# An interleave kernel on one core: rows of 32 KiB in double buffers, loads issued from GpSimd with joined descriptors asked for

## The chip, the cores and the metric

The kernel runs on one core of a Trainium2 chip. The metric is device time in microseconds, the median of several executions. The profile's span is shorter than this time by 1.8 to 2.6 us. Ratios are the mean time of one kernel's fast runs over that of the other's fast runs of the same rounds, so they are not quite the ratios of the medians quoted.

## The reference

```python
batch, seq, dim = 32, 256, 1024
# x, y: float32 (batch, seq, dim)
result[..., 0::2] = x
result[..., 1::2] = y        # float32 (batch, seq, 2 * dim)
```

No arithmetic is done: 67.11 MB are read and 67.11 MB written, in another order.

## The kernel before

The flat arrays are cut into tiles of 128 rows. SyncE issues the loads of x and y, VectorE copies each into every second element of an output tile, ScalarE issues the store.

```python
WL = 4096                    # columns of a load tile: rows of 16 KiB
WS = 2048                    # columns of x per output tile: output rows of 16 KiB
xpool = ctx.enter_context(tc.tile_pool(name="xp", bufs=3))
ypool = ctx.enter_context(tc.tile_pool(name="yp", bufs=3))
opool = ctx.enter_context(tc.tile_pool(name="op", bufs=6))
lwidths = [WL] * (total // P // WL - 1) + [2048, 1024, 512, 256, 256]
for lw in lwidths:
    ...
    nc.sync.dma_start(out=xtile, in_=xs)
    nc.sync.dma_start(out=ytile, in_=ys)
    while soff < lw:
        ...
        nc.vector.tensor_copy(out=otile[:, 0::2], in_=xsub)
        nc.vector.tensor_copy(out=otile[:, 1::2], in_=ysub)
        nc.scalar.dma_start(out=os_, in_=otile)
```

The last widths shrink, so that little stands alone at the end: the last load, its copies, the last store.

Of the kernel before, what the change touches and what calls it, by code (L numbers as in the profile page):

```python
# [2 lines left out]

# [4 lines left out]


@with_exitstack
def kernel(
    ctx: ExitStack,
    tc: tile.TileContext,
    x: bass.AP,
    y: bass.AP,
    out: bass.AP,
):
    nc = tc.nc
    P = 128  # L20

    total = 1
    for s in x.shape:
        total *= s

    WL = 4096
    WS = 2048

    xf = x.rearrange("b s d -> (b s d)")
    yf = y.rearrange("b s d -> (b s d)")  # L30
    of = out.rearrange("b s d -> (b s d)")

    fp32 = mybir.dt.float32

    xpool = ctx.enter_context(tc.tile_pool(name="xp", bufs=3))
    ypool = ctx.enter_context(tc.tile_pool(name="yp", bufs=3))
    opool = ctx.enter_context(tc.tile_pool(name="op", bufs=6))

    lwidths = [WL] * (total // P // WL - 1) + [2048, 1024, 512, 256, 256]
    assert sum(lwidths) == total // P  # L40

    start = 0
    k = 0
    for lw in lwidths:
        xtile = xpool.tile([P, WL], fp32, name="xtile")[:, :lw]
        ytile = ypool.tile([P, WL], fp32, name="ytile")[:, :lw]

        xs = dataclasses.replace(xf, offset=start, ap=[[lw, P], [1, lw]])
        ys = dataclasses.replace(yf, offset=start, ap=[[lw, P], [1, lw]])
        nc.sync.dma_start(out=xtile, in_=xs)  # L50
        nc.sync.dma_start(out=ytile, in_=ys)  # L51

        soff = 0
        while soff < lw:
            width = min(WS, lw - soff)
            otile = opool.tile([P, 2 * WS], fp32, name="otile")[:, : 2 * width]
            os_ = dataclasses.replace(
                of,
                offset=2 * start + 2 * soff,
                ap=[[2 * lw, P], [1, 2 * width]],  # L60
            )
            xsub = xtile[:, soff : soff + width]
            ysub = ytile[:, soff : soff + width]
            if False:
                nc.gpsimd.tensor_copy(out=otile[:, 0::2], in_=xsub)
                nc.gpsimd.tensor_copy(out=otile[:, 1::2], in_=ysub)
            else:
                nc.vector.tensor_copy(out=otile[:, 0::2], in_=xsub)  # L68
                nc.vector.tensor_copy(out=otile[:, 1::2], in_=ysub)  # L69
            nc.scalar.dma_start(out=os_, in_=otile)  # L70
            k += 1
            soff += width

        start += P * lw
    assert start == total


# [1 line left out]
_INS = ['x', 'y']  # L79
_OUTS = [((32, 256, 2048), 'float32')]  # L80


# [23 lines left out]
```

## Time and profile before

| | before |
|---|---|
| time, median (four runs) | 319.75 us |
| span of the profiled run | 317.6 us |
| first data packet, last packet ends (us into the span) | 1.73, 315.96 |
| DMA bytes, mean rate | 134.24 MB, 423 GB/s |
| VectorE busy | 24% |

The rows of the page that carry the bound stand in the prediction below. Between the first and the last packet lie 314.2 us. So nearly all of the time is data moving, and 3.4 us of the span are start and end. The chances of a change lie in the cost per packet (8.4 ns by the prediction's fit), in these edges, and in not making holes.

### The profile page before, as it was taken

The numbers are of one execution on the slowest core, as the hardware profiler recorded it, in microseconds if no ns is written. First come the engines' busy times: TensorE is split into PE (matmuls) and PEld (weight loads), VectorE is DVE, ScalarE is ACT, GpSimd is POOL, SyncE is SP. The second block draws the span as 40 slices with busy tenths as digits, with TensorE's granted clock in tenths as the row PEclk, the third lists the DMA queues.
The fourth block names the chain that finished last, engine by engine and source line by source line (L and its number), as shares of the span: only waits on it lengthen the run. The fifth ranks groups of instructions, "written<-read, shape, count | busy, mean of one in ns | idle before, by whom it ended". The sixth has DMA issues, their size and how long they took to land.

```text
span 317.6 us, 285 instructions
## 1 busy us (share of the span) xinstructions
DVE 76.8 (24%) x70; POOL 0.2 (0%) x4
## 2 busy tenths in 40 slices
DVE  0522112222022221122220222202222202221130
POOL 0000000000000000000000000000000000000000
DMA  8999999999999999999999999999999999999997
GB/s 293 429 396 429 429 431 429 429 429 437 437 435 433 433 429 429 429 429 429 429 431 429 429 429 435 437 437 430 431 431 429 431 429 429 429 432 427 421 423 285
DMA packets 10802, 134.24 MB, mean 423 GB/s; under 512 B 1200, under 2 KB 1712, under 8 KB 2608
## 3 DMA queue, kind: packets, MB, share of 16 engines
q1 hardware_dynamic: 5760, 67.11, 50.0%
q10 hardware_dynamic: 5040, 67.11, 49.4%
q14 instruction: 2, 0.02, 0.0%
HBM read 67.11 MB, written 67.11 MB: 423 GB/s over the span
## 4 chain that ended last, share of the span: by engine, by line
DMA 94%; issue 3%; SPq 1%; DVE 1%
DMA xtile<-in_x_dram 82%; DMA ytile<-in_y_dram 12%; SPq L51 0%; DVE otile L69 0%; SPq L50 0%; DVE otile L68 0%
## 5 line engine op out<-in xcount | busy, mean ns | idle before, releaser
L68 DVE COPY otile<-xtile 128x2048 f32<-128x2048 f32 (+3 forms) x35 | 38.4, 1134 | 118.4 <-issue 94.4
L69 DVE COPY otile<-ytile 128x2048 f32<-128x2048 f32 (+3 forms) x35 | 38.4, 1134 | 117.9 <-DMA ytile<-in_y_dram 117.9
L90 POOL MEMSET const-bfloat16-1.0<- 128x1 bf16 x1 | 0.1, 102 | 0.0
L90 POOL MEMSET const-uint8-127<- 128x1 uint8 x1 | 0.1, 101 | 0.0
L90 POOL MEMSET const-float32-0.0<- 128x1 f32 x1 | 0.1, 99 | 0.2 <-issue 0.2
L90 POOL MEMSET const-float32-1.0<- 128x1 f32 x1 | 0.1, 98 | 0.0
## 6 DMA issues: line engine op xcount, KB each, us to landing
out_dram<-otile ACTq DMA_DIRECT2D x31, 2048.0 KB, 19.5
xtile<-in_x_dram SPq DMA_DIRECT2D x15, 2048.0 KB, 38.8
ytile<-in_y_dram SPq DMA_DIRECT2D x15, 2048.0 KB, 38.8
xtile<-in_x_dram SPq DMA_DIRECT2D x1, 1024.0 KB, 36.4
ytile<-in_y_dram SPq DMA_DIRECT2D x1, 1024.0 KB, 34.0
out_dram<-otile ACTq DMA_DIRECT2D x1, 1024.0 KB, 9.2
xtile<-in_x_dram SPq DMA_DIRECT2D x1, 512.0 KB, 29.0
ytile<-in_y_dram SPq DMA_DIRECT2D x1, 512.0 KB, 30.2
```

The source lines that it names most:

```text
L68: nc.vector.tensor_copy(out=otile[:, 0::2], in_=xsub)
L69: nc.vector.tensor_copy(out=otile[:, 1::2], in_=ysub)
L90: nc = _bacc.Bacc("TRN2", target_bir_lowering=False, num_devices=1)
```

## The change

The intent: longer rows mean fewer descriptors; the memory stays the same (192 KiB per partition) because triple and sixfold buffering become double; loads leave SyncE for GpSimd, where `single_packet=True` asks for descriptors to be joined.

```diff
-    WL = 4096
-    WS = 2048
+    WL = 8192
+    WS = 4096
...
-    xpool = ctx.enter_context(tc.tile_pool(name="xp", bufs=3))
-    ypool = ctx.enter_context(tc.tile_pool(name="yp", bufs=3))
-    opool = ctx.enter_context(tc.tile_pool(name="op", bufs=6))
+    xpool = ctx.enter_context(tc.tile_pool(name="xp", bufs=2))
+    ypool = ctx.enter_context(tc.tile_pool(name="yp", bufs=2))
+    opool = ctx.enter_context(tc.tile_pool(name="op", bufs=2))
...
-    lwidths = [WL] * (total // P // WL - 1) + [2048, 1024, 512, 256, 256]
+    lwidths = [WL] * (total // P // WL - 1) + [4096, 2048, 1024, 512, 512]
...
-        nc.sync.dma_start(out=xtile, in_=xs)
-        nc.sync.dma_start(out=ytile, in_=ys)
+        nc.gpsimd.dma_start(out=xtile, in_=xs, single_packet=True)
+        nc.gpsimd.dma_start(out=ytile, in_=ys, single_packet=True)
```

(A counter and a branch that was never taken are removed too; they leave no instruction.)

More of the change, by code (lines that the diff above doesn't have):

```diff
@@ L33 @@
     fp32 = mybir.dt.float32
-    xpool = ctx.enter_context(tc.tile_pool(name="xp", bufs=3))
-    ypool = ctx.enter_context(tc.tile_pool(name="yp", bufs=3))
-    opool = ctx.enter_context(tc.tile_pool(name="op", bufs=6))
-    lwidths = [WL] * (total // P // WL - 1) + [2048, 1024, 512, 256, 256]
+    xpool = ctx.enter_context(tc.tile_pool(name="xp", bufs=2))
+    ypool = ctx.enter_context(tc.tile_pool(name="yp", bufs=2))
+    opool = ctx.enter_context(tc.tile_pool(name="op", bufs=2))
+    lwidths = [WL] * (total // P // WL - 1) + [4096, 2048, 1024, 512, 512]
     assert sum(lwidths) == total // P
     start = 0
-    k = 0
     for lw in lwidths:
@@ L63 @@
             ysub = ytile[:, soff : soff + width]
-            if False:
-                nc.gpsimd.tensor_copy(out=otile[:, 0::2], in_=xsub)
-                nc.gpsimd.tensor_copy(out=otile[:, 1::2], in_=ysub)
-            else:
-                nc.vector.tensor_copy(out=otile[:, 0::2], in_=xsub)
-                nc.vector.tensor_copy(out=otile[:, 1::2], in_=ysub)
+            nc.vector.tensor_copy(out=otile[:, 0::2], in_=xsub)
+            nc.vector.tensor_copy(out=otile[:, 1::2], in_=ysub)
             nc.scalar.dma_start(out=os_, in_=otile)
-            k += 1
             soff += width
```

## The prediction

> **What bounds the kernel now.** I read the page's first three parts, then the stretches of the span (windows), the order of instructions in the middle (timeline), what DVE waits for, and last the single packet records of the DMA queues in the trace.
>
> ```profile
> DVE 76.8 (24%) x70; POOL 0.2 (0%) x4
> DMA  8999999999999999999999999999999999999997
> GB/s 293 429 396 429 429 431 429 429 429 437 437 435 433 433 429 429 429 429 429 429 431 429 429 429 435 437 437 430 431 431 429 431 429 429 429 432 427 421 423 285
> q1 hardware_dynamic: 5760, 67.11, 50.0%
> q10 hardware_dynamic: 5040, 67.11, 49.4%
> ```
>
> The row DMA is the busy share of the 16 DMA engines in tenths, 40 slices of the span. It is full in all slices but the first and the last, and the rate under it stays near 430 GB/s. Queue q1 holds the loads, q10 the stores: 50.0% and 49.4% add up to 99.4% of the engines' time. VectorE works 24% of the span. So the kernel is bound by DMA, without holes to fill.
>
> ```profile
> 100.00:200.00 100.00, 23.64 (x20) 0.00 (x0) 1.00 1.01 432
> 200.00:290.00 90.00, 22.51 (x19) 0.00 (x0) 1.00 1.00 430
> 310.00:318.00 8.00, 0.29 (x1) 0.00 (x0) 1.00 0.68 276
> ```
>
> The last two columns are DMA share and GB/s: 1.00 or 1.01 in the long middle. Only the last 8 us are partly empty (0.68).
>
> ```profile
> 57.75 0.33 SPq L50 DMA_DIRECT2D xtile<-in_x_dram  x1
> 57.77 2.36 DVE L68 COPY otile<-xtile 128x2048 f32<-128x2048 f32 x2 [7.42 <-issue]
> 67.44 2.37 DVE L69 COPY otile<-ytile 128x2048 f32<-128x2048 f32 x2 [7.31 <-DMA ytile<-in_y_dram]
> ```
>
> VectorE does two copies of x in 2.36 us, then is idle over 7 us until y is there. Its waits are the consequence of the DMA bound, not a cause.
>
> **The floor, from packet sizes.** In the trace a packet of 1 KiB took 46 ns, 2 KiB 84, 4 KiB 159, 8 KiB 309, 16 KiB 611 (medians, alike in both queues). The slope is (611-46)/(16384-1024) ns per byte, or 27.2 bytes per ns; the rest is 611-602.6 = 8.4 ns for each packet. A semaphore write is a packet of its own, 9 ns. One engine carries 8 of a tile's 128 rows. Before: 40 loads and 35 stores, 75 DMAs x 8 rows = 600 data packets per engine. Bytes: 134.22 MB/16/27.2 = 308.4 us; fixed: 600 x 8.4 ns = 5.0 us; semaphores: 75 x 9 ns = 0.7 us; together 314.1 us. In the trace the first data packet starts 1.7 us into the span and the last packet ends at 316.0: 314.2 us. The model fits and there is no idle in it. The remaining 1.7 us are the end of the program. The reported 319.8 us is 2.2 us above the span of 317.6.
>
> [...]16 x 27.2 bytes per ns is 435 GB/s, and 430 is reached with the packets' fixed cost in it.[...] q1 and q10 each get half.[...] Here the first SyncE load was issued at 0.73 us and moved at 1.73, so 1.0 us; nothing in this trace shows GpSimd.[...] The copies do run[...] (2048 elements in 1225 ns, 1024 in 697: 0.52 ns per element)[...].
>
> **The change, part by part.** The bytes are the same. *Rows of 32 KiB:* now 12 widths, so 24 loads, and 14+5 = 19 stores; 43 DMAs x 8 = 344 row descriptors per engine instead of 600. Fixed cost 344 x 8.4 ns = 2.9 us and semaphores 0.4 us: DMA work 308.4+2.9+0.4 = 311.7 us, a gain of **2.4 us**. If joined descriptors share one fixed cost, the loads' 192 x 8.4 ns = 1.6 us goes too, at most. *VectorE:* half the instructions of double size; about 1225 + 2048 x 0.52 = 2290 ns each, 4.6 us for an x and y pair. It stays at a quarter of the span.[...]
>
> *Double buffers:* the middle worked as a timetable. Loads have run ahead and wait; two output buffers are being stored, and store A ends at time 0. Store B then occupies the engines until 9.7. Meanwhile VectorE sees A's semaphore (0.4 us, as the first x load's last semaphore write to its copy, 8.09 to 8.48 us), refills A (4.6), and the new store's first packet starts about 1.4 us after (estimate, a bit above SyncE's 1.0 at the start): 6.4 us. So there is always a store to move, with 3.3 us to spare. When B is refilled too, x and y come free and two loads follow[...]. A period is 4 x 9.7 = 38.8 us for 16 MiB, without a hole. The engines' spread at the end of a load or store is up to 1.9 us in the trace (27.71 to 29.61 us for the semaphore writes of the first store), which leaves 1.4 us. **No idle in the middle, but thin.**
>
> *Tail:* the last stores of 4096, 2048, 1024, 512, 512 columns go through two buffers, no longer six. If the 4096 one ends at T, those of 2048 and 1024 end at T+4.9 and T+7.3. The next needs the buffer of the 2048 one: 4.9+0.4+0.9 (two short copies)+1.4 = T+7.6, so 0.3 us of idle; it ends at T+8.9. The last needs the buffer freed at T+7.3: +2.7 = T+10.0, 1.1 us more. With the spread between engines I take **+2.5 us**. The end of the program stays 1.7 us.
>
> Sum: 3.0 + 311.7 + 2.5 + 1.7 = 318.9 us of span, + 2.2 = **321.1 us**. I round up to 321.5 for small holes in the middle.
>
> **Rivals.** *A: no buffer stall at all, only the gain in descriptors.* The fit of 314.1 against 314.2 speaks for it; the later start and the two output buffers against. It makes 319.8-2.4 = 317.4 us, or 316 with the joined fixed cost. Even this is not 2% faster (313.4), as the bytes alone need 308.4 us. *B: the double buffer becomes the wait.* Slack is 3.3 us per period[...]. There are about 7 periods; 2 us lost in each makes 14 us, about 335 us. For it speaks the arithmetic of thin slack[...]; against it that stores are always queued at the boundaries in my timetable. *C: GpSimd's path is slower itself*[...]: 2% on the loads' half costs 3 us, about 325. [...]I hold it unlikely.
>
> **Range and chances.** A and the plain sum span 316 to 322, a mild B or C reaches 328. I give 318 to 328 for 8 in 10. Faster by 2% would need DMA above 435 GB/s or nearly so: 0.02. Slower by 2%, above 326.2 us, needs B or a strong C: 0.19. Else the same: 0.79.
>
> **What the changed profile would show.** Right: DMA at 9 in all middle slices, at most 2 or 3 us of holes, all near the end; 32 KiB packets of 1.21 us; loads and stores alternating in bursts rather than half and half; first packet near 3 us; VectorE still near 25%, now waiting for output buffers (stores) rather than for y. Wrong: slices of 7 or 8 in the middle once per 38.8 us (B), packets longer than 1.22 us or one DMA engine behind the others (C), or a start later than 4 us. What would overturn it most is loads crowding out stores so that the two output buffers stand waiting while the loads have nowhere to land.

The prediction's sum came to 3.0 + 311.7 + 2.5 + 1.7 = 318.9 us of span, 321.1 us of time, rounded up to 321.5. Its first term: a start at 3.0 us, 1.3 later than the 1.7 of before. An assumption changed no term of the sum, only the order: that loads from GpSimd take longer turns than stores and so run ahead. The timetable of the double buffers starts from it. Its 9.7 us for a load or a store are 8 rows of 1.213 us (32768 bytes at 27.2 per ns, and 8.4 ns).

## The result, and the profile after

The changed kernel takes **321.64 us** (321.47 to 321.81, four runs) against 319.75 us: ratio 1.0059, 95% interval 1.0045 to 1.0074. That is 1.9 us slower, and "the same" at 2%. The profiled run has a span of 319.1 us.

The page of the changed kernel: busy time of the compute engines, DMA share and rate in 40 slices, queues (q0 now holds the loads).

```profile
DVE 73.6 (23%) x38; POOL 22.6 (7%) x28
DMA  6999999999999999999999999999999999999996
GB/s 263 456 419 370 448 419 444 448 411 448 415 448 448 407 448 415 448 448 411 448 415 444 444 419 448 415 444 431 431 448 411 429 431 439 458 423 413 396 379 250
q0 software_dynamic: 3200, 67.11, 49.4%
q10 hardware_dynamic: 2736, 67.11, 49.1%
```

The DMA row is 9 everywhere but at the edges, as before; the first slice fell from 8 to 6, the last from 7 to 6. The last three rates (396, 379, 250) are lower than those of before (421, 423, 285). A single slice of the middle says little: a row of 1.2 us is booked where it starts.

What engines wait for, changed kernel:

```profile
POOL xtile L49 <- DVE otile L63: 258.7, 9, 44.6
DVE otile L63 <- DMA out_dram<-otile: 182.3, 15, 23.5
DVE otile L64 <- DMA ytile<-in_y_dram: 35.4, 10, 7.6
```

VectorE now waits mostly for output buffers, that is for stores to finish (182.3 us in 15 waits), no longer for y. With the DMA engines full (share 1.00 from 40 to 240 us, below) this waiting costs nothing by itself.

To see where time came from, take the same stretches of both kernels. Columns: stretch and length, busy time of VectorE and of GpSimd with instruction counts, clock, DMA share, GB/s. First the kernel before:

```profile
3.00:40.00 37.00, 11.18 (x10) 0.00 (x0) 1.00 1.00 421
40.00:240.00 200.00, 47.91 (x41) 0.00 (x0) 1.00 1.01 431
240.00:290.00 50.00, 13.05 (x11) 0.00 (x0) 1.00 1.00 428
290.00:300.00 10.00, 1.23 (x1) 0.00 (x0) 1.00 1.01 429
300.00:310.00 10.00, 3.08 (x7) 0.00 (x0) 1.00 1.02 415
310.00:315.00 5.00, 0.29 (x1) 0.00 (x0) 1.00 1.01 413
```

Then the changed kernel:

```profile
3.00:40.00 37.00, 8.99 (x4) 1.55 (x3) 1.00 0.99 414
40.00:240.00 200.00, 45.45 (x20) 12.78 (x10) 1.00 1.00 433
240.00:290.00 50.00, 13.68 (x6) 3.62 (x4) 1.00 1.01 433
290.00:300.00 10.00, 1.23 (x1) 0.54 (x1) 1.00 0.97 414
300.00:310.00 10.00, 2.62 (x3) 2.15 (x3) 1.00 0.99 376
310.00:315.00 5.00, 1.36 (x4) 0.00 (x0) 1.00 0.94 389
```

The rates show where to look: less at the start, a little more in the middle, less after 290 us, where the tiles shrink (the tail). For amounts they are too coarse, as the view books a row where it starts, and one row of 32 KiB on each of 16 engines is 0.5 MB, or 1.2 us. So the packet records of both traces were counted, each row by the part of it that had moved. Put into time at 431 GB/s, the changed kernel is 0.9 us behind at 40 us and 0.3 us ahead at 290 us. Its last packet ends 1.6 us later (317.57 against 315.96 us). So the start lost about 0.9 us, the middle won about 1.1, and **the tail lost about 1.9 us**. Counted from the end, the last 10 MB took 26.2 us, in the kernel before 24.3.

Two details of the changed kernel's trace. First, GpSimd's issues beside a copy, in the middle (start, length, engine; in brackets the idle time before it and what ended it):

```profile
73.32 2.29 DVE L64 COPY otile<-ytile 128x4096 f32<-128x4096 f32 x1
73.70 2.02 POOL L49 DMA_DIRECT2D xtile<-in_x_dram  x1 [44.64 <-DVE otile L63]
75.91 0.53 POOL L50 DMA_DIRECT2D ytile<-in_y_dram  x1 [0.18 <-issue]
```

GpSimd is free to issue x's load at 73.70, when the copy of x is done, but VectorE is copying y until 75.61; GpSimd's instruction ends 0.11 us after that and lasts 2.02 us, where the undisturbed one lasts 0.53. All six issues of the trace that met a copy of 4096 columns lasted 2.02 to 2.03 us. They cost nothing visible here: from 40 to 240 us the rate is 433 GB/s, as in the run with loads from SyncE.

Second, the tail:

```profile
301.09 1.23 DVE L64 COPY otile<-ytile 128x2048 f32<-128x2048 f32 x1 [7.64 <-DMA ytile<-in_y_dram]
302.39 0.69 DVE L63 COPY otile<-xtile 128x1024 f32<-128x1024 f32 x1
303.59 0.69 DVE L64 COPY otile<-ytile 128x1024 f32<-128x1024 f32 x1 [0.50 <-DMA ytile<-in_y_dram]
310.25 0.43 DVE L63 COPY otile<-xtile 128x512 f32<-128x512 f32 x1 [5.97 <-DMA out_dram<-otile]
310.69 0.43 DVE L64 COPY otile<-ytile 128x512 f32<-128x512 f32 x1
314.49 0.43 DVE L63 COPY otile<-xtile 128x512 f32<-128x512 f32 x1 [3.38 <-DMA out_dram<-otile]
314.84 0.42 DVE L64 COPY otile<-ytile 128x512 f32<-128x512 f32 x1
```

The last two copies of x each begin when a store has freed one of the two output buffers: in the trace the stores of 2048 and 1024 columns are seen as landed at 310.13 and 314.37 us. The last two loads of y are seen as landed at 310.66 and 314.26, at nearly the same moments, so a second wait ends beside the first. The last x and y are issued late, at 303.38 and 304.58 us, because the copies of 1024 columns free their input buffers only at 303 to 304 us. These copies did not wait for an output buffer: the store of 4096 columns is seen as landed at 300.39 us. They stood in VectorE's order behind the copy of the y of 2048 columns, which landed at 301.06, and then their own x and y landed at 302.31 and 303.56. The last store is issued at 315.29 us, when the rows of the one before have ended; no row moves from 315.05 until 316.14 us. That is the hole foreseen, 1.1 us. One more loss shows there: between 303 and 310 us the 16 KiB rows of a store took 611 to 1208 ns, median 663, where such a row took 611 in the kernel before (median). In the stretch from 305 to 310 us this adds up to 0.9 us per engine.

### The profile page after: what moved, and what is told of

Same layout as the page of the kernel before. It is cut to its first block, busy times and chain, and to the rows that moved or that the text cites. A ratio compares the mean times of both kernels' runs of the same rounds, so it can differ in the third digit from the quotient of the medians.

```text
span 319.1 us, 178 instructions
## 1 busy us (share of the span) xinstructions
DVE 73.6 (23%) x38; POOL 22.6 (7%) x28
## 2 busy tenths in 40 slices
DMA packets 5936, 134.22 MB, mean 421 GB/s; under 512 B 688, under 2 KB 688, under 8 KB 1456
## 3 DMA queue, kind: packets, MB, share of 16 engines
q10 hardware_dynamic: 2736, 67.11, 49.1%
## 4 chain that ended last, share of the span: by engine, by line
DMA 62%; issue 34%; DVE 1%; POOL 1%; DVEq 0%; POOLq 0%; PEldq 0%
DMA xtile<-in_x_dram 37%; DMA ytile<-in_y_dram 22%; DMA out_dram<-otile 3%; DVE otile L64 1%; POOL xtile L49 1%; POOL ytile L50 0%; DVE otile L63 0%; DVEq L95 0%; POOLq L49 0%; DVEq L63 0%; POOLq L50 0%; PEldq L95 0%
## 5 line engine op out<-in xcount | busy, mean ns | idle before, releaser
L63 DVE COPY otile<-xtile 128x4096 f32<-128x4096 f32 (+3 forms) x19 | 37.1, 1958 | 206.3 <-DMA out_dram<-otile 182.3
L64 DVE COPY otile<-ytile 128x4096 f32<-128x4096 f32 (+3 forms) x19 | 37.1, 1956 | 35.4 <-DMA ytile<-in_y_dram 35.4
L49 POOL DMA_DIRECT2D xtile<-in_x_dram x12 | 16.0, 1332 | 259.7 <-DVE otile L63 258.7
L50 POOL DMA_DIRECT2D ytile<-in_y_dram x12 | 6.4, 536 | 22.6 <-DVE otile L64 21.4
```

The lines of the kernel that those rows point to most:

```text
L49: nc.gpsimd.dma_start(out=xtile, in_=xs, single_packet=True)
L50: nc.gpsimd.dma_start(out=ytile, in_=ys, single_packet=True)
```

## The experiments

Costs in microseconds against the kernel before are (ratio - 1) x 319.6 of each run's own rounds. The whole change costs 1.9 by the same rule.

### Without the joining

```diff
-        nc.gpsimd.dma_start(out=xtile, in_=xs, single_packet=True)
+        nc.gpsimd.dma_start(out=xtile, in_=xs)      # y alike
```

> The changed kernel without the joining of an engine's descriptors. Theory A (the joining doesn't alter whose turn it is: an engine changes queue after every row anyway): 321.6 us within 0.4, and the first store still ends near 51 us of the span with loads and stores at half the rate each in the middle. Theory B (the joining gives loads longer turns than stores): the first store would end earlier without it than the 51.3 us of the changed kernel, and the time would move by more than 1 us.

Measured: 321.74 us, ratio 1.0058 (1.0042 to 1.0074), cost 1.9: as the whole change. The packets in the trace are the same in number and size (3200 and 2736). In both, the first store moves from about 31 us to its last semaphore write (a packet of 4 bytes and 9 ns; 1200 for the 75 transfers before the change, 688 for the 43 after it) at 51.3 us (changed kernel) or 49.3 us (this one) beside loads, and then x and y land alternately every 19.36 us: 16 rows of 1.21 us. Between 60 and 66 us the number of engines that move a load row swings from 16 to 0 and back every 2.4 us, in both traces. So loads and stores took turns **row by row, joined or not**. The joining had no visible effect; Theory A. One execution of the six, the profiled one, took 319.98 us, the others 321.35 to 321.93. In its middle the 16 engines finished a transfer within 0.5 us of each other, in the changed kernel's trace within 1.2 (loads) and 2.3 us (stores). Its last 10 MB took 24.8 us, not 26.2, with the same two output buffers. So what two buffers cost at the tail is not fixed. The slower executions of this run have no trace; that the engines' spread makes the 1.7 us is only argued.

### The two halves of the change alone

Rows and buffers alone (loads from SyncE):

```diff
-        nc.gpsimd.dma_start(out=xtile, in_=xs, single_packet=True)
+        nc.sync.dma_start(out=xtile, in_=xs)        # y alike
```

> The changed kernel with loads issued from SyncE. Theory A (GpSimd costs only its later start): the first load packet at 1.7 us instead of 2.6, span and time shorter by 0.9 us, so about 320.5 us (319.9 to 320.9). Theory B (GpSimd also costs in the middle[...]): shorter by 2 us or more, 319.6 or less. Theory C (the start is hidden elsewhere): no change.

GpSimd alone (the kernel before, its loads as in the change):

```diff
-        nc.sync.dma_start(out=xtile, in_=xs)
+        nc.gpsimd.dma_start(out=xtile, in_=xs, single_packet=True)   # y alike
```

> The kernel before with its loads issued from GpSimd, joined; rows of 16 KiB and the buffers of before. Theory A (later start alone): span longer by 0.9 us, time 320.6 to 321.1. Theory B ([...]with 16 KiB rows there are twice as many issues): over 322. If this part costs about as much as the whole change (1.9 us), then rows and buffers together are worth nothing, as the 2.4 us of fewer descriptors are given back at the tail.

Measured: rows and buffers alone 318.95 us, ratio 0.9981 (0.9969 to 0.9993), 0.6 us **faster** than before; GpSimd alone 320.61 us, ratio 1.0035 (1.0022 to 1.0048), 1.1 slower. In the traces the first packet comes at 1.72 and 2.63 us. So GpSimd alone costs about its later start, 0.9 us, as Theory A of that run said. But -0.6 and +1.1 make +0.5, and the whole costs +1.9: the two halves together lose another 1.4 us. About 0.5 of this lies outside the profiles' spans: time less span is 2.6 us in the changed kernel, 2.2 with SyncE loads, 1.8 with GpSimd alone and 1.9 in the kernel before. Taking GpSimd out of the changed kernel won 2.5 to 2.7 us, which Theory B of that run expected for a wrong reason: GpSimd's longer issues (2.02 us, above) didn't slow the middle (433 GB/s from 40 to 240 us in both).

### Where GpSimd's other cost lies: first loads, last loads

```diff
+        if start == 0:                              # e7: first two loads
+        if lw < WL:                                 # e8: the ten narrow last loads
+            nc.sync.dma_start(...)                  # x and y
+        else:
             nc.gpsimd.dma_start(..., single_packet=True)
```

> The changed kernel with the first two loads alone issued from SyncE. SyncE for all loads won 2.7 us, though the first packet came only 0.9 us earlier. Theory A (all of the loss is made at the start, where the engines fall out of step by one row, which then lasts to the end): 318.7 to 319.5. Theory B (the start is worth its 0.9 us and the rest is lost at the tail): 320.4 to 321.0.

> The changed kernel with the ten loads of the five narrow last widths issued from SyncE, the fourteen large ones still from GpSimd. Theory A of the run before (the start does it all): no change, 321.3 to 321.9. Theory B (the tail is where GpSimd costs the other 1.8 us): 319.6 to 320.3.

Measured for the last loads from SyncE: 320.58 us, ratio 1.0025 (1.0012 to 1.0038), cost 0.8. So issuing the last loads from GpSimd costs about **1.1 us**. The time lies between the ranges of the two theories, and Theory A is out. With the start it makes 0.9 + 1.1 = 2.0 of the 2.5; another 0.4 is outside the span (2.6 against 2.2 us). That the gain was made in the tail is inferred from the edit: the profiled execution was the slowest of the five (321.33 us), and its last 10 MB took 26.6 us. The run with all loads from SyncE does show a shorter tail, 25.3 us. By which mechanism GpSimd's last loads cost more is open.

Measured for the first loads from SyncE: 324.99 us, ratio 1.0161, cost 5.1. Both theories missed. The edit changed more than the start: the second tile's loads, on the other queue, now took turns with the first tile's, so the first x landed at 19.9 instead of 13.7 us, and the first store was issued at 42 instead of 26 us. Later the engines drifted apart: they finished one load within 0.7 us of each other at first, only within about 4 us by the end of the middle; rows took longer, and the tail held holes. As a test of the start it is void.

### More VectorE work: is the double buffer thin?

```diff
             nc.vector.tensor_copy(out=otile[:, 0::2], in_=xsub)
             nc.vector.tensor_copy(out=otile[:, 1::2], in_=ysub)
+            nc.vector.tensor_copy(out=otile[:, 0::2], in_=xsub)
+            nc.vector.tensor_copy(out=otile[:, 1::2], in_=ysub)
```

> The changed kernel with each pair of copies done twice (same result): 4.6 us more VectorE time per output tile. Theory A (turns row by row, an output buffer is refilled some 11 to 14 us ahead of its turn): no hole in the middle, only the tail pays about 1 to 3 us, so 322.5 to 325. Theory B (the timetable of the prediction, 3.3 us to spare per store with loads running ahead): at least 1.3 us of hole in each of 7 to 14 turns, 331 us or more.

Measured: ratio 1.0374, cost 12.0; the two fast executions took 331.15 and 331.94 us, two slow ones 337.18 and 338.21. The time fits Theory B, the trace does not: from 40 to 290 us there are no holes worth naming. There, the rate fell from 433 to 425 GB/s because rows took longer than 1213 ns, and the rest went in the tail, where the engines finished one load up to 13.6 us apart, against 0.6 us at first. One might think that VectorE slows the DMA. Against that: in the changed kernel, between 50 and 245 us, rows that overlapped a copy took the same time as rows that didn't, to 0.1 ns in the mean. In this run also rows that overlapped no copy were longer, by 17 ns, and those more than half within copies by 26. What sets the engines apart was not settled.

### Small buffers of their own for the last stores

```diff
+    tpool = ctx.enter_context(tc.tile_pool(name="tp", bufs=3))
...
-            otile = opool.tile([P, 2 * WS], ...)[:, : 2 * width]
+            if lw <= 512: otile = tpool.tile([P, 1024], ...)[:, : 2 * width]
+            else:         otile = opool.tile([P, 2 * WS], ...)[:, : 2 * width]
```

> The changed kernel, with three small output buffers of their own for the last two widths (512 columns), so that the last two stores wait for no earlier store. Theory A (the hole of about 1.3 us before the last store is the wait for the buffer of the store before the previous one): that hole goes, 0.8 to 1.8 us faster than the changed kernel, so 319.9 to 320.9. Theory B (the last loads come late and set the end anyway): within 0.4 us of the changed kernel's 321.6.

> The same small buffers, with the loads issued from SyncE: rows of 32 KiB kept, both costs taken out. If start and tail costs add up, it is 0.8 to 1.5 us under the 318.95 us of the run with SyncE loads alone: 317.4 to 318.2, and below both kernels. If the last loads set the end: 318.6 to 319.2.

Measured: 325.21 us (ratio 1.0173), and with loads from SyncE 321.66 us (1.0071): slower than without these buffers by 3.6 and 2.7 us of median. Both theories missed. The tail of the run with loads from GpSimd shows why:

```profile
310.22 0.43 DVE L69 COPY ttile<-ytile 128x512 f32<-128x512 f32 x1 [5.66 <-DMA ytile<-in_y_dram]
313.69 0.43 DVE L69 COPY ttile<-ytile 128x512 f32<-128x512 f32 x1 [2.42 <-DMA ytile<-in_y_dram]
314.03 0.69 DVE L68 COPY otile<-xtile 128x1024 f32<-128x1024 f32 x1
```

With buffers of their own, the 512-column copies stand ahead of the 1024-column copies in VectorE's order. The copies of 1024 columns, whose data were there, began at 314.03 us, after the copy of the very last y (313.69). From 310 to 315 us DMA stood at a share of 0.22. The experiment does not answer its question, and shows that here the added buffers changed the order of instructions too.

### The number of output buffers

The same memory as four buffers of 16 KiB rows keeps the order, as all outputs come from one pool.

```diff
-    WS = 4096
+    WS = 2048
-    opool = ctx.enter_context(tc.tile_pool(name="op", bufs=2))
+    opool = ctx.enter_context(tc.tile_pool(name="op", bufs=4))   # e12: bufs=2 kept
```

> The changed kernel with the same four output buffers of 16 KiB rows, loads from GpSimd. Theory A (output buffers make the holes): 320.3 to 321.2, against 321.6 for the changed kernel. Theory B (late last loads): 322.4 to 323.2.

> The changed kernel with two output buffers of 16 KiB rows; the run with four of them took 319.6 us, 2.0 less than the changed kernel. Theory A (the number of output buffers made that gain: with four, a store needn't wait for the one before the last): with two the holes of about 2 us at the tail stay and 1.2 us of descriptors come on top, and with stores of 4.9 us against some 4.3 us to refill (0.4 to see the semaphore, 2.45 of copies, 1.4 to the first packet) there may be holes in the middle too: 322.5 us or more. Theory B (shorter store rows, which change the order at the tail, made it): 319.3 to 320.3.

Measured: four buffers 319.60 us, ratio 1.0001 (0.9989 to 1.0012), cost 0.0: **all of the change's loss is gone**, though stores have more descriptors and loads still start late. Two buffers of the same size: 332.81 us, ratio 1.0392, cost 12.5 (one slow execution, 336.69 us, left out). Theory A both times, with more effect than expected. For the tail the traces compare more directly: the last 10 MB took 26.2 us in the changed kernel, 23.8 with four buffers of 16 KiB rows, and 26.2 with two of them. So the shorter row alone brings nothing at the tail; **the number of output buffers** does. These are single traced executions, and the one without joining, 24.8 us with two large buffers, shows that they vary. Four buffers of 32 KiB rows were not tried. The stretches of the run with four buffers, to be held against those of the changed kernel:

```profile
40.00:240.00 200.00, 46.71 (x40) 6.23 (x9) 1.00 1.00 431
240.00:290.00 50.00, 16.55 (x15) 4.72 (x7) 1.00 1.01 431
300.00:310.00 10.00, 1.55 (x3) 0.54 (x1) 1.00 0.99 420
310.00:315.00 5.00, 0.86 (x2) 0.00 (x0) 1.00 0.95 394
```

The middle gives back 2 GB/s of 433 (a load row and two short store rows, 1213 + 2 x 611 ns, instead of 2 x 1213 would make 1.6, an estimate), and the stretch from 300 to 310 us moves 420 instead of 376 GB/s. The last packet ends at 315.72 us, not 317.57. With four buffers the last two copies of x wait for their loads and no longer for a store:

```profile
310.88 0.43 DVE L63 COPY otile<-xtile 128x512 f32<-128x512 f32 x1 [2.10 <-DMA xtile<-in_x_dram]
```

The loads before come sooner as well: the y of 2048 columns landed at 289.39 us, not 301.06. The copies of 1024 columns begin at 295.57 us for x and 301.63 for y instead of 302.39 and 303.59, so the last x and y are issued at 296.56 and 302.62 instead of 303.38 and 304.58, and the last store at 313.44 instead of 315.29. With two small buffers the DMA row itself has holes:

```profile
DMA  7999999999999999999999999999997999899995
40.00:240.00 200.00, 47.28 (x40) 7.44 (x10) 1.00 1.00 418
240.00:290.00 50.00, 13.04 (x12) 1.49 (x2) 1.00 0.93 389
```

Slices of 7 and 8 stand in the last third, where the prediction's rival of the double buffer as the wait would have put them all through. From 40 to 240 us the engines are full (share 1.00), yet the rate is 418 GB/s, as rows took longer by 5.6 us per engine in sum. Later there are holes too. That a store of 4.9 us does not cover some 4.3 us of refilling plus the engines' spread fits the holes, but was not shown for each; why the rows were longer is open. Most of the 12.5 us is lost before the tail.

### Four output buffers with loads from SyncE

```diff
-        nc.gpsimd.dma_start(out=xtile, in_=xs, single_packet=True)
+        nc.sync.dma_start(out=xtile, in_=xs)        # y alike; WS = 2048, op bufs=4
# e11, in addition:
-    ... [4096, 2048, 1024, 512, 512]
+    ... [4096, 2048, 1024, 512, 256, 256]
```

> Loads from SyncE in rows of 32 KiB, but output in four buffers of 16 KiB rows (the memory of the two of 32 KiB). Stores then have 280 row descriptors per engine instead of 152 (1.1 us more at 8.4 ns) and 16 more semaphore writes (0.1 us). Theory A (two output buffers cost about 2 us of holes at the tail): those go, so 0 to 0.8 us faster than the 318.95 of the run with SyncE loads: 318.1 to 318.9. Theory B (the tail's holes come from the late last loads, not from the buffers): 1.2 us slower, 319.8 to 320.5.

> Four output buffers, loads from SyncE, and the end cut finer: 512, 256, 256 columns where the run with four buffers has 512, 512. The last load and the last store are half as long, about 1 us less that stands alone at the end; five more semaphore writes and 24 more descriptors cost 0.3 us. If the last load's landing and the last store set the end: 0.3 to 0.8 us faster than with four buffers. If the fixed latency of each step does: same or slower by up to 1 us.

Measured: 322.23 us (ratio 1.0075) and, with the finer end, 321.40 us (1.0071). Both are slower than the 318.95 us of two large buffers from SyncE; neither theory of the first had this. (It counted 280 descriptors for the stores; 34 stores make 272. The finer end adds three semaphore writes, not five.) The finer end is 0.8 us faster by medians and 0.1 by ratios, and its six executions lie between 320.32 and 324.00 us, so it decides nothing. The tail of the first run did gain: its last 10 MB took 24.5 us, against 25.3 with two large buffers. The loss lies earlier. In the trace the rows of the first run took 5.0 us per engine more in total than their size asks (8.4 ns + bytes/27.2), against 1.5 us in the run with four buffers from GpSimd. The excess falls where the loads had run dry and begin again beside stores, near 126, 206 and 274 us, each about 0.7 to 1.7 us. From GpSimd the same restart cost nothing. Why is open.

## Why the prediction was right

The prediction was 321.5 us, range 318 to 328, "same" most likely; 321.64 came. It is right in the main terms, with two steps wrong (the turns of loads and stores, and the way through the tail) and a lucky sum.

- **DMA is the bound, and bytes set a floor: right.** No run of the fourteen kernels came below 318.7 us.
- **Fewer descriptors, 2.4 us: right in kind, too large.** 32 KiB rows took 1213 ns, the figure foreseen; 8.4 ns + bytes/27.2 fits the medians of all rows from 1 to 32 KiB in both traces but the 16 KiB store rows of the changed kernel's tail. But the middle, 250 of the 314 us, won about 1.1 us, where 2.4 in all would make 1.9. The prediction's fit of 314.1 to 314.2 us was partly luck: in the kernel before the records add up to 316.0 us per engine, as rows, mostly in the first 40 us, took 1.9 us more than their size asks. They fit into 314.2 us because records of one engine overlap. So a packet costs less elapsed time than its 8.4 ns, some 6 ns (an estimate: 1.8 us of overlap over 675 packets).
- **Start, +1.3 us (not shown by a trace beforehand): a little large.** The first packet came at 2.61 us, +0.9; from the first load's instruction to it passed 1.4 us with GpSimd (1.25 to 2.61) and 1.0 with SyncE (0.73 to 1.73); the run of GpSimd alone gives 1.1 in all.
- **Longer turns for loads (the assumption above): wrong.** Loads and stores took turns row by row, half and half and not in bursts, in the trace and in the run without joining. The timetable built on it, with loads running ahead and 3.3 us to spare, did not take place: in the middle a refilled store is issued 11 to 14 us before its turn (issued at 75.64 us, its turn at about 90).
- **No idle in the middle: right**, by a larger margin than argued. How close two buffers are to the edge, the run with two 16 KiB buffers shows at half the row.
- **Tail, +2.5 us: near in size (1.9), half right in its path.** The last two copies of x did begin when a store had freed a buffer, and the last hole was 1.1 us, as foreseen. That the number of output buffers matters, the runs with four and with two of them show. But between the ends of the stores of 4096 and 2048 columns lie 9.7 us (300.39 and 310.13 us), where the prediction had 4.9: the second store had to wait for its y, which landed at 301.06, and its rows took up to 1208 ns. Late loads and longer rows were not in the sum.
- **Rivals.** A (no stall) was short of the late start and the tail. B did not happen with rows of 32 KiB. C (GpSimd's path slower itself) is out for the middle; that the last loads cost 1.1 us more from GpSimd may be a form of it, which is not shown.
- **The sum was lucky.** The start was put 0.4 us too high, the tail 0.6, the gain in the middle 0.8: these cancel in part. From the traces, start +0.9, first to last packet +0.7 and end -0.1 make the span 1.5 us longer; the time rose by 1.9. The remaining 0.4 us lie outside the span, where the trace shows nothing; the 0.4 us of rounding up, meant for small holes in the middle, happened to cover it.

A small gain was to be had: rows and buffers with loads left on SyncE, 318.95 us, beat both kernels, by 0.2% and 0.8%.

## What to carry to other kernels

When the DMA engines are full from end to end, as here (share 1.00 from 40 to 240 us), count bytes and packets first: what was left to win here was per-packet cost and the two edges, and the change that trades buffers for longer rows won about 1.1 us in the middle and lost about 1.9 in the last few small transfers. Here two output buffers left no hole in the middle with stores of 9.7 us; with stores of 4.9 us, and at the shrinking tail, they did. When an experiment adds a buffer, look at the order of the instructions before you read its time.
